# Rotary embedding on one core: the tables' loads moved to the GpSimd queue, and the fp32 head widened from two positions to four

## The chip, the core and the metric

The kernel runs on one core of one Trainium2 chip. The time is in device microseconds of one execution; the figure before is the median of three runs, 317.81 us (317.26 to 318.22). Engines are named as in the profile: DVE is VectorE, ACT is ScalarE, POOL is GpSimd, SP is SyncE. DMAs are issued by SP (queue q1, "hardware_dynamic", in the profile) and by POOL (queue q0, "software_dynamic"); both queues' packets run on the same 16 DMA engines.

## What is computed

An interleaved rotary embedding of x with 8 batches, 2048 positions, 16 heads and 64 elements per head, all float32 in HBM. The tables cos and sin have 2048 x 32 elements.

```python
x_pairs = x.reshape(batch, seq_len, num_heads, head_dim // 2, 2)
x1 = x_pairs[..., 0]
x2 = x_pairs[..., 1]
out1 = x1 * cos - x2 * sin
out2 = x1 * sin + x2 * cos
out = np.stack([out1, out2], axis=-1)
```

x is 67.1 MB and so is the output; each table is 0.26 MB.

## The kernel before

One batch is one tile of 128 partitions. Partition p holds 16 consecutive positions (K = 16) of 1024 elements each, so its row in HBM is 64 KB of float32. The tile `xt` in SBUF is bfloat16: the load (L56, `load`) and the store (L59, `store`) are DMAs issued by POOL which cast on the way, 64 KB of float32 on one side and 32 KB of bfloat16 on the other. There are five such tiles (NX = 5), for eight batches.

`rotate(b, k0, k1)` does the arithmetic on positions k0 to k1 of batch b with three DVE instructions: x times the sine table into the scratch tile `qt` (L74), x times the cosine table in place (L75), and the sum with the pairs of `qt` swapped (L80). The tables `s_tab` and `c_tab` are made once from `sin_sb` and `cos_sb` by three short DVE instructions (L93 to L95), the sine with the alternating sign.

The first positions of batch 0 go another way: SP loads them as float32 into the staging tile `head` (L84), and ACT casts them into the first tile (L91). HEAD is the number of these positions. Load 0 on POOL's queue brings the others. The last four positions of the last batch (TAIL = 4) go out in the same manner: ACT casts them to float32 (L118) and SP stores them (L119). `head`, `tail` and every `qt` share one buffer (tag "work").

The order is written out by hand. SP issues the head, then cos, then sin. POOL issues loads 0 to 4 without waiting. Then it goes batch by batch: store b waits for the rotation of batch b. After store 0, POOL runs a copy of one element (L106, `mark`) that reads the tile of load 4 and so waits for its landing; stores 1 and later are issued behind it. From batch 1 on, a load of batch b + 4 follows store b; it reuses the tile of batch b - 1 and waits on POOL until that batch's store has landed. So the issues run: loads 0 to 4, store 0, mark, store 1, load 5, store 2, load 6, store 3, load 7, stores 4 to 7. The last store leaves out the tail, and ACT's one-element copy (L117) holds the tail back until store 6 has landed.

In terms of rows: a transfer over 128 partitions puts eight rows on each of the 16 DMA engines. A row of a plain load is 64 KB on the HBM side, of load 0 it is 56 KB, of the head 8 KB, of a table 2 KB, of the tail 16 KB. Beside its 128 rows each transfer has 16 short completion packets, one for each engine: 16 transfers on POOL's queue give 16 x 144 = 2304 packets.

Of the kernel before, what the change touches and what calls it, by code (L numbers as in the profile page):

```python
# [2 lines left out]

# [4 lines left out]


@with_exitstack  # L10
def kernel(
    ctx: ExitStack,
    tc: tile.TileContext,
    x: bass.AP,
    cos: bass.AP,
    sin: bass.AP,
    out: bass.AP,
):
    nc = tc.nc
    fp32 = mybir.dt.float32  # L20
    bf16 = mybir.dt.bfloat16
    mult = mybir.AluOpType.mult
    add = mybir.AluOpType.add

    B, S, H, D = x.shape
    P = 128
    K = S // P
    KP = 16
    D2 = D // 2
    HD = H * D  # L30
    NX = 5
    HEAD = 2
    TAIL = 4


    x_t = x.rearrange("b (p k) h d -> b p k (h d)", p=P, k=K)
    out_t = out.rearrange("b (p k) h d -> b p k (h d)", p=P, k=K)
    cos_t = cos.rearrange("(p k) c -> p (k c)", p=P, k=K)
    sin_t = sin.rearrange("(p k) c -> p (k c)", p=P, k=K)

    consts = ctx.enter_context(tc.tile_pool(name="consts", bufs=1))
    xpool = ctx.enter_context(tc.tile_pool(name="xpool", bufs=NX))
    stage = ctx.enter_context(tc.tile_pool(name="stage", bufs=1))

    cos_sb = consts.tile([P, K * D2], fp32)
    sin_sb = consts.tile([P, K * D2], fp32)
    c_tab = consts.tile([P, K, D], bf16)
    s_tab = consts.tile([P, K, D], bf16)

    mark = consts.tile([1, 1], bf16)  # L50
    tiles = {}

    def load(b, k0=0):
        if b not in tiles:
            tiles[b] = xpool.tile([P, K, HD], bf16, name="xt")
        nc.gpsimd.dma_start(out=tiles[b][:, k0:], in_=x_t[b, :, k0:])  # L56

    def store(b, k1=K):
        nc.gpsimd.dma_start(out=out_t[b, :, :k1], in_=tiles[b][:, :k1])  # L59

    def rotate(b, k0, k1):
        nk = k1 - k0
        xp = tiles[b][:, k0:k1]
        qt = stage.tile([P, KP, HD], bf16, name="qt", tag="work")

        def rows(a):
            return a.rearrange("p k (h e) -> p k h e", h=H, e=D)

        def tab(a):
            return dataclasses.replace(  # L70
                a, offset=a.offset + k0 * D, ap=[a.ap[0], [D, nk], [0, H], [1, D]]
            )

        nc.vector.tensor_tensor(out=rows(qt[:, :nk]), in0=rows(xp), in1=tab(s_tab), op=mult)  # L74
        nc.vector.tensor_tensor(out=rows(xp), in0=rows(xp), in1=tab(c_tab), op=mult)  # L75
        q_swap = dataclasses.replace(
            qt, offset=qt.offset + 1, ap=[qt.ap[0], [2, nk * HD // 2], [-1, 2]]
        )
        x3 = xp.rearrange("p k (a j) -> p (k a) j", j=2)
        nc.vector.tensor_tensor(out=x3, in0=x3, in1=q_swap, op=add)  # L80

    with tc.manual_schedule():
        head = stage.tile([P, TAIL, HD], fp32, name="st", tag="work")
        nc.sync.dma_start(out=head[:, :HEAD], in_=x_t[0, :, :HEAD])  # L84
        nc.sync.dma_start(out=cos_sb, in_=cos_t)
        nc.sync.dma_start(out=sin_sb, in_=sin_t)
        load(0, HEAD)
        for b in range(1, NX):
            load(b)

        nc.scalar.copy(out=tiles[0][:, :HEAD], in_=head[:, :HEAD])  # L91
        s2 = s_tab.rearrange("p k (i j) -> p (k i) j", j=2)
        nc.vector.tensor_copy(out=s2[:, :, 0], in_=sin_sb)  # L93
        nc.vector.tensor_scalar_mul(s2[:, :, 1], sin_sb, -1.0)  # L94
        nc.vector.tensor_copy(  # L95
            out=c_tab.rearrange("p k (i j) -> p (k i) j", j=2),
            in_=cos_sb.to_broadcast([P, K * D2, 2]),
        )
        for b in range(B):
            if b == 0:  # L100
                rotate(b, 0, HEAD)
                rotate(b, HEAD, KP)
            else:
                rotate(b, 0, KP)
            if b == 1:
                nc.gpsimd.tensor_copy(out=mark, in_=tiles[NX - 1][:1, K - 1, :1])  # L106
            if b < B - 1:
                store(b)

            if b >= 1 and b - 1 + NX < B:  # L110
                load(b - 1 + NX)
        store(B - 1, K - TAIL)

        tail = stage.tile([P, TAIL, HD], fp32, name="st", tag="work")
        nc.scalar.copy(out=tiles[B - 2][:1, 0, :1], in_=tiles[B - 1][:1, K - 1, :1])  # L117
        nc.scalar.copy(out=tail, in_=tiles[B - 1][:, K - TAIL :])  # L118
        nc.sync.dma_start(out=out_t[B - 1, :, K - TAIL :], in_=tail)  # L119


# [1 line left out]
_INS = ['x', 'cos', 'sin']  # L123
_OUTS = [((8, 2048, 16, 64), 'float32')]


# [23 lines left out]
```

## Time and profile before

| | before |
|---|---|
| median of the runs | 317.81 us (317.26 to 318.22) |
| span of the profiled execution | 315.5 us |
| bytes read from and written to HBM | 67.63 MB and 67.11 MB, 427 GB/s over the span |
| DVE busy | 210.3 us, 67% of the span |
| ACT busy, POOL busy | 6.9 us, 11.7 us |
| head issued, landing after | 0.74 us, 4.7 us |
| cos issued, landing after | 1.16 us, 13.4 us |
| sin issued, landing after | 1.63 us, 31.7 us |
| load 0 issued, landing after | 1.24 us, 22.3 us |
| first DVE instruction | 33.38 us |
| store 0 issued | 61.93 us |
| L74, L75, L80 on a whole batch | 8.69 us each |
| tail issued, landing after | 299.08 us, 15.5 us |

The profiler records one execution. Times of issue are taken from its timeline; "landing" is the time from issue until the semaphore of the transfer shows it complete. In the view of the DMAs, a stretch of time can be given, and it then counts the packets that start there, with their bytes on the writing side and the time they take as a share of 16 engines over that stretch. A share can be over 100% where long packets start in a short stretch.

### The profile page before, as it was taken

The numbers are of one execution on the slowest core, as the hardware profiler recorded it, in microseconds if no ns is written. First come the engines' busy times: TensorE is split into PE (matmuls) and PEld (weight loads), VectorE is DVE, ScalarE is ACT, GpSimd is POOL, SyncE is SP. The second block draws the span as 40 slices with busy tenths as digits, with TensorE's granted clock in tenths as the row PEclk, the third lists the DMA queues.
The fourth block names the chain that finished last, engine by engine and source line by source line (L and its number), as shares of the span: only waits on it lengthen the run. The fifth ranks groups of instructions, "written<-read, shape, count | busy, mean of one in ns | idle before, by whom it ended". The sixth has DMA issues, their size and how long they took to land.

```text
span 315.5 us, 125 instructions
## 1 busy us (share of the span) xinstructions
DVE 210.3 (67%) x30; ACT 6.9 (2%) x4; POOL 11.7 (4%) x21
## 2 busy tenths in 40 slices
DVE  0000799999999999999999993899509994000000
ACT  4000000000000000000000000000000000000400
POOL 3000000000000301010000100000000000000000
DMA  9899999999999999999999999999999999999997
GB/s 279 184 261 206 199 220 245 199 199 253 212 199 266 399 449 482 399 332 245 220 399 399 399 199 199 399 532 266 199 241 490 399 399 490 440 399 399 432 432 332
DMA packets 2880, 101.71 MB, mean 322 GB/s; under 512 B 320, under 2 KB 320, under 8 KB 576
## 3 DMA queue, kind: packets, MB, share of 16 engines
q0 software_dynamic: 2304, 98.04, 97.1%
q1 hardware_dynamic: 576, 3.67, 3.0%
HBM read 67.63 MB, written 67.11 MB: 427 GB/s over the span
## 4 chain that ended last, share of the span: by engine, by line
another core or an unknown queue 91%; DMA 1%; ACTq 1%; ACT 1%; issue 0%
DMA st<-in_x_dram 1%; ACTq L145 1%; ACT xt L91 1%; ACT xt L117 0%; ACTq L117 0%
## 5 line engine op out<-in xcount | busy, mean ns | idle before, releaser
L74 DVE TENSOR_TENSOR qt<-xt,s_tab 128x16384 bf16<-128x16384 bf16 (+2 forms) x9 | 69.7, 7743 | 19.1 <-DMA xt<-in_x_dram 18.8
L75 DVE TENSOR_TENSOR xt<-xt,c_tab 128x16384 bf16<-128x16384 bf16 (+2 forms) x9 | 69.7, 7743 | 0.4
L80 DVE TENSOR_TENSOR xt<-xt,qt 128x16384 bf16<-128x16384 bf16 (+2 forms) x9 | 69.7, 7744 | 0.3
L93 DVE CAST s_tab<-sin_sb 128x512 bf16<-128x512 f32 x1 | 0.5, 453 | 33.4 <-DMA sin_sb<-in_sin_dram 33.4
L59 POOL DMA_DIRECT2D out_dram<-xt x8 | 4.3, 534 | 139.9 <-DVE xt L80 139.9
L56 POOL DMA_DIRECT2D xt<-in_x_dram x8 | 4.4, 560 | 72.8 <-DMA out_dram<-xt 72.0
L117 ACT COPY xt<-xt 1x1 bf16<-1x1 bf16 x1 | 0.2, 192 | 288.0 <-DMA out_dram<-xt 288.0
L106 POOL COPY mark<-xt 1x1 bf16<-1x1 bf16 x1 | 2.9, 2929 | 39.6 <-DMA xt<-in_x_dram 39.6
L118 ACT CAST st<-xt 128x4096 f32<-128x4096 bf16 x1 | 3.6, 3598 | 0.0
L91 ACT CAST xt<-st 128x2048 bf16<-128x2048 f32 x1 | 1.9, 1897 | 3.4 <-DMA st<-in_x_dram 3.4
L91 ACT ACT_TABLE_LOAD x1 | 1.3, 1283 | 0.7 <-PEq L134 0.7
L95 DVE CAST c_tab<-cos_sb 128x1024 bf16<-128x1024 f32 x1 | 0.7, 683 | 0.0
L94 DVE TENSOR_SCALAR s_tab<-sin_sb 128x512 bf16<-128x512 f32 x1 | 0.4, 444 | 0.0
L134 POOL MEMSET const-float32-0.0<- 128x1 f32 x1 | 0.1, 100 | 0.2 <-issue 0.2
L134 POOL MEMSET const-bfloat16-1.0<- 128x1 bf16 x1 | 0.1, 102 | 0.0
L134 POOL MEMSET const-float32-1.0<- 128x1 f32 x1 | 0.1, 100 | 0.0
L134 POOL MEMSET const-uint8-127<- 128x1 uint8 x1 | 0.1, 100 | 0.0
## 6 DMA issues: line engine op xcount, KB each, us to landing
xt<-in_x_dram POOLq DMA_DIRECT2D x7, 4096.0 KB, 57.6
out_dram<-xt POOLq DMA_DIRECT2D x1, 6144.0 KB, 47.8
xt<-in_x_dram POOLq DMA_DIRECT2D x1, 3584.0 KB, 22.3
out_dram<-st SPq DMA_DIRECT2D x1, 2048.0 KB, 15.5
st<-in_x_dram SPq DMA_DIRECT2D x1, 1024.0 KB, 4.7
cos_sb<-in_cos_dram SPq DMA_DIRECT2D x1, 256.0 KB, 13.4
sin_sb<-in_sin_dram SPq DMA_DIRECT2D x1, 256.0 KB, 31.7
out_dram<-xt POOLq DMA_DIRECT2D x7, 70.1
```

What stands on the lines that cost most here:

```text
L56: nc.gpsimd.dma_start(out=tiles[b][:, k0:], in_=x_t[b, :, k0:])
L59: nc.gpsimd.dma_start(out=out_t[b, :, :k1], in_=tiles[b][:, :k1])
L74: nc.vector.tensor_tensor(out=rows(qt[:, :nk]), in0=rows(xp), in1=tab(s_tab), op=mult)
L75: nc.vector.tensor_tensor(out=rows(xp), in0=rows(xp), in1=tab(c_tab), op=mult)
L80: nc.vector.tensor_tensor(out=x3, in0=x3, in1=q_swap, op=add)
L91: nc.scalar.copy(out=tiles[0][:, :HEAD], in_=head[:, :HEAD])
L93: nc.vector.tensor_copy(out=s2[:, :, 0], in_=sin_sb)
L94: nc.vector.tensor_scalar_mul(s2[:, :, 1], sin_sb, -1.0)
L95: nc.vector.tensor_copy(out=c_tab.rearrange("p k (i j) -> p (k i) j", j=2), in_=cos_sb.to_broadcast([P, K * D2, 2]),)
L106: nc.gpsimd.tensor_copy(out=mark, in_=tiles[NX - 1][:1, K - 1, :1])
L118: nc.scalar.copy(out=tail, in_=tiles[B - 1][:, K - TAIL :])
L145: with _tile.TileContext(nc) as tc:
```

## The change

Two things are changed. HEAD goes from 2 to 4, so that the head's rows are 16 KB and load 0's are 48 KB, ACT's cast covers four positions, and batch 0 is rotated as positions 0 to 4 and 4 to 16. And the loads of cos and sin are issued by POOL, after load 0 and ahead of loads 1 to 4, where before SP issued them behind the head. SP then issues the head alone until the tail at the end.

```diff
     HD = H * D
     NX = 5
-    HEAD = 2
+    HEAD = 4
     TAIL = 4
...
         head = stage.tile([P, TAIL, HD], fp32, name="st", tag="work")
         nc.sync.dma_start(out=head[:, :HEAD], in_=x_t[0, :, :HEAD])
-        nc.sync.dma_start(out=cos_sb, in_=cos_t)
-        nc.sync.dma_start(out=sin_sb, in_=sin_t)
         load(0, HEAD)
+        nc.gpsimd.dma_start(out=cos_sb, in_=cos_t)
+        nc.gpsimd.dma_start(out=sin_sb, in_=sin_t)
         for b in range(1, NX):
             load(b)
```

## The prediction

> **What bounds the kernel.** I first read the page's slices and queue totals. The DMA line shows the 16 engines full from the first slice to the last, and the two queues' shares add up to 97.1% + 3.0%. No compute engine comes near: DVE works 67% of the span and is done at about 263 us.
>
> ```profile
> DVE  0000799999999999999999993899509994000000
> DMA  9899999999999999999999999999999999999997
> q0 software_dynamic: 2304, 98.04, 97.1%
> q1 hardware_dynamic: 576, 3.67, 3.0%
> ```
>
> Next the waits, to see who is kept waiting by what, and then the timeline of POOL, which issues nearly every transfer.
>
> ```profile
> DVE s_tab L93 <- DMA sin_sb<-in_sin_dram: 33.4, 1, 33.4
> POOL mark L106 <- DMA xt<-in_x_dram: 39.6, 1, 39.6
> ...
> 61.93 0.54 POOL L59 DMA_DIRECT2D out_dram<-xt  x1 [57.89 <-DVE xt L80]
> 102.11 2.93 POOL L106 COPY mark<-xt 1x1 bf16<-1x1 bf16 x1 [39.64 <-DMA xt<-in_x_dram]
> 104.98 0.54 POOL L59 DMA_DIRECT2D out_dram<-xt  x1
> 121.68 0.53 POOL L56 DMA_DIRECT2D xt<-in_x_dram  x1 [16.17 <-DMA out_dram<-xt]
> ```
>
> The 33.4 us that DVE waits for sin look like the prize, but they are not on the path. Store 0 is issued at 61.93, behind loads 1 to 4 in q0's order. Load 4 lands at 102.1, and store 0, the only other work queued, lands at 121.68, that is 19.6 us later: the time one whole batch takes. So store 0 sat ready for 40 us, and DVE could be 40 us later, or any amount earlier, without moving it. From there on each batch costs the same: stores 4, 5 and 6 end a stretch from 237.26 to 295.28, 58.02 / 3 = 19.34 us each; loads 1 to 2 land 19.35 us apart (issues at 1.91 and 2.45, landing 41.1 and 59.9 later). The end is therefore the start of the stream plus the work of all packets in it. Only what happens before load 4 lands can change, and it moves the end one for one.
>
> **How an engine's time is spent at the start.** Asking the DMA view for short stretches gives packets by the time at which they start; share times stretch times 16 engines over packets is the length of one.
>
> ```profile
> q1 hardware_dynamic: 99, 0.81, 98.1%
> q1 hardware_dynamic: 35, 0.07, 87.2%
> q0 software_dynamic: 16, 0.46, 96.8%
> q1 hardware_dynamic: 16, 0.03, 4.4%
> q0 software_dynamic: 16, 0.52, 243.2%
> q1 hardware_dynamic: 26, 0.43, 99.3%
> q0 software_dynamic: 15, 0.49, 310.1%
> ```
>
> In order: 2.5 to 4.5 us, the head's 8 KB rows, 0.981 x 2 x 16 / 99 = 0.317 us each. 5.0 to 5.2, the tables' 2 KB rows back to back, 0.872 x 0.2 x 16 / 35 = 0.080 us (33 of the 35 are table rows, so 0.097 by count). 16.0 to 18.2, load 0 beside cos: each engine takes one 56 KB row (2.13 us) and one 2 KB row (0.097 us) in turn, 2.2 us a pair. 37 to 38, plain loads, 64 KB rows at 2.43 us. 311 to 312, the last store's 16 KB rows on the SP queue, 0.611 us. 98 to 99, the last packets of load 4, 3.3 us instead of 2.43: a single hitch of 0.9 us, whose cause no row shows. Every size runs close to one rate, 64 KB in 2.42 us.
>
> The turns explain sin's lateness: with load packets in q0, each 2 KB row on the SP queue waits out one large row. That is also why they cost little: an engine is never empty.
>
> **The change part by part**, per DMA engine, eight rows of every transfer each, from the first SP packet (about 2.0 us, mean over the engines) to the end of load 4.
>
> 1. Head of 4 positions. Removed: 8 rows of 8 KB, 8 x 0.317 = 2.54 us. Added: 8 rows of 16 KB at the tail's price, 8 x 0.611 = 4.89 us. Net +2.35. Low bound for 16 KB: the pace of 64 KB, 0.605; high bound, twice an 8 KB row, 0.634. So +2.30 to +2.53.
> 2. Load 0 shrinks from 56 to 48 KB rows: 8 x 8 KB, at the load pace exactly one 64 KB row, -2.42 us (bounds -2.41 from the spacing, -2.43 from the packet). With part 1: -0.07, bounds -0.13 to +0.12. The same bytes cross; only the queue differs.
> 3. The tables. Before, 16 rows per engine: some 5 in the gap between head and load 0 at 0.08 to 0.097, 11 in turn with load rows at about 0.09 (the pair of 2.2 us less the 2.11 that a 56 KB row takes at the load pace) or 0.06 (beside 64 KB rows: 2.47 less 2.41). Sum about 5 x 0.09 + 8 x 0.09 + 3 x 0.06 = 1.35 us. After, all 16 back to back in q0 between load 0 and load 1: 16 x 0.097 = 1.55. Bounds: 16 x 0.06 = 0.96 and, if the hardware queue's pace does not carry over, 16 x 0.12 = 1.92 (0.65 us from the last head row to the first load row for some 5.5 table rows). Net +0.2, bounds -0.4 to +0.6.
> 4. Two more transfers in q0, so two more ends of a transfer. At the ends of loads 1 to 3 none is seen: the 16 completion packets and the next load's 16 first rows start in the same stretch (42 to 43 us). The other end is the hitch of 0.9 us where load 4 meets store 0. I take 0.1 each, near the first row because these are loads followed by loads; bounds 0 and 1.8 for both.
> 5. POOL issues two more DMAs between load 0 and load 1, at 0.56 us each; loads 1 to 4 are issued 1.1 us later, the last at some 5.2 us instead of 4.04. Load 0 keeps the engines until about 21 us. Nothing; without that cover it would be 1.1 us. SP loses two issues (0.42 each), ahead of nothing. Should load 0's first packet, now at 5.35 on average, come 1.1 us later, the larger head alone fills the engines to 2.0 + 4.89 = 6.9.
> 6. ACT's copy of the head (L91) goes from 1.9 to 3.6 us, the time of the same size in L118; rotations of 4 and 12 positions replace 2 and 14, for the same total. The head now shares its engines with 48 KB rows from 5.35 on: about 5.3 of its 8 rows are done, the rest wait out one load row each, 2.7 x 2.4, so it lands near 12.5 us. Load 0 lands near 22, sin near 24, and DVE starts some 9 us earlier than 33.4. All of this lies under the queue of loads that ends at 102; cover gone, the ACT copy would cost 1.7 us.
>
> The queue's price deserves a rule that speaks against the change. The rows above show no gap at a load's end on q0. The Trainium skill, "DMA: Bandwidth & Descriptors", section "Anatomy of one DMA - SWDGE (gpsimd) path", gives each GpSimd DMA a fixed 2.0 us beside its bytes, mostly the receipt of the last write. If the tables paid it in a row with the loads, an estimate by that page is 4 us more for the two, near 322 us. The rows disagree: 19.35 us from load to load, the pace of the packets alone, leaves no room for such a cost between queued transfers.
>
> **Sum.** -0.07 + 0.2 + 0.2 = +0.3 us. The profiled span is 315.5 us, and the median of the runs is 317.81, 2.3 above it, the launch's share that the change doesn't touch. 317.81 + 0.3 = 318.1. From the bounds: -0.13 - 0.4 + 0 = -0.5, to 0.12 + 0.6 + 1.8 = +2.5.
>
> **Rivals.**
> - The tables drag (slower). Place: q0 between load 0 and load 1, 16 short rows with nothing on the SP queue to fill in, and two ends of transfers. For it: the hitch at 98 us and the dip to 22.1% share at 4.8 us where head gives way to cos; against it: clean ends at loads 1 to 3. It decides from the point where parts 3 and 4 exceed 1.0 us together; with 1.92 - 1.35 + 0.9 for one hitch, +1.5: 319.3 us.
> - The start gains (faster). Larger rows fill the early gap better, the tables run at 0.06, and the hitch at load 4 (0.9 us, shown once) doesn't return: -0.5 - 0.9 = -1.4, 316.4 us. Against it: the hitch lies where reads turn to writes, which the change leaves.
> - DVE's 9 us count (much faster). If the wait for sin were on the path, the time would fall toward 309 us. Against it: store 0 waits 40 us in the queue, and at 19.34 us a batch, 16 batches' worth of bytes take 309.4 us alone, before a start of 2.0, the 0.5 MB of tables, and 2.3 around the span.
> - It doesn't do what it says: the head is not sped up by being alone, since load 0's rows alternate with it. Likely, and the time is that of the forecast.
>
> **Numbers.** What a measurement here can tell from no change is about 0.3%, 0.95 us: 316.86 to 318.76. The forecast, including the last rival, 0.60; the tables drag 0.26; the start gains 0.11; DVE counts 0.03. The forecast's own range, with the runs' spread of half a us, is 317.2 to 318.9. For 8 in 10 I go from 316.7, inside the gain, to 319.5, past one hitch. Slower 0.27 (the drag and the forecast's upper edge), faster 0.14, same 0.59.
>
> **What would show it.** Sin landing near 24 us and the first DVE instruction with it, load 1 landing within 1 us of 43.0, load 4 within 1 us of 102.1, store 0 still landing 19.6 us after it: then the steps hold. A gap of more than 0.1 us per table row, or empty engines between load 0's last row and load 1's first, shows the drag. The prediction is wrong altogether if the pace of 19.34 us per batch changes, or if load 0 begins so late that the engines stand empty before it.

## The result

In the first comparison, 21 runs of each, the changed kernel took 317.31 us (317.12 to 317.51) and the kernel before 317.75 us (317.26 to 318.45): a ratio of 0.9983, 95% interval 0.9977 to 0.9989. That is inside the 0.3% called "no change" in the prediction and inside its range, but it is 0.44 us on the faster side, where the sum had +0.3 us. Five later comparisons on the same two kernels gave 0.9999, 1.0001, 1.0000, 0.9991 and 0.9991. The changed kernel stood between 317.29 and 317.43 us in all six; it is the kernel before that moved, from 317.31 to 317.75.

The profile after, first the page's slices and queue totals (digits are tenths of a slice; queues give packets, MB, share of 16 engines):

```profile
DVE  0009999999999999999879960799509994000000
DMA  7999999999999999999999999999999999999997
q0 software_dynamic: 2464, 98.04, 96.7%
q1 hardware_dynamic: 288, 4.19, 3.4%
```

The engines are as full as before, the shares add up to 100.1% again, and the span is 315.5 us, the same as that of the profile before. DVE starts a slice and more earlier and stands idle later instead. The waits (total, times, longest) and POOL's timeline say where:

```profile
POOL mark L106 <- DMA xt<-in_x_dram: 49.2, 1, 49.2
DVE qt L74 <- DMA xt<-in_x_dram: 28.5, 3, 12.6
DVE s_tab L93 <- DMA sin_sb<-in_sin_dram: 23.8, 1, 23.8
```

```profile
52.40 0.54 POOL L59 DMA_DIRECT2D out_dram<-xt  x1 [47.27 <-DVE xt L80]
...
102.18 2.06 POOL L106 COPY mark<-xt 1x1 bf16<-1x1 bf16 x1 [49.24 <-DMA xt<-in_x_dram]
104.18 0.54 POOL L59 DMA_DIRECT2D out_dram<-xt  x1
...
122.05 0.53 POOL L56 DMA_DIRECT2D xt<-in_x_dram  x1 [17.34 <-DMA out_dram<-xt]
```

In the kernel before, the line of the waits of L74 for loads was

```profile
DVE qt L74 <- DMA xt<-in_x_dram: 18.8, 2, 12.4
```

DVE's wait for sin shrank from 33.4 to 23.8 us, and its waits for loads grew from 18.8 to 28.5 us: the 9.6 us it gained at the start it gave back, to a tenth, further on. Store 0 is issued 9.5 us earlier and changes nothing, because load 4 lands at 102.18 (before: 102.11) and store 0 lands after it, at 122.05 (before: 121.68).

The issues of the first loads, with KB each and the time to landing:

```profile
xt<-in_x_dram POOLq DMA_DIRECT2D x1, 3072.0 KB, 21.2
st<-in_x_dram SPq DMA_DIRECT2D x1, 2048.0 KB, 14.5
...
cos_sb<-in_cos_dram POOLq DMA_DIRECT2D x1, 256.0 KB, 21.3
sin_sb<-in_sin_dram POOLq DMA_DIRECT2D x1, 256.0 KB, 21.4
```

Issued at 0.73, the head lands at 15.2 us, where before it landed at 5.4: alone on its queue, it waits for load 0's rows all the same. Cos and sin, issued by POOL at 1.90 and 2.44, land right behind load 0, at 23.2 and 23.8 us.

Short stretches of the DMA view, packets by their start: 3.5 to 5.1 us, 16.3 to 18.1 us and 21.9 to 22.9 us.

```profile
q1 hardware_dynamic: 45, 0.74, 110.8%
q0 software_dynamic: 16, 0.39, 101.6%
DMA packets 124, 0.40 MB, mean 397 GB/s; under 512 B 27, under 2 KB 27, under 8 KB 124
q0 software_dynamic: 124, 0.40, 99.7%
```

The head's 16 KB rows take 1.108 x 1.6 x 16 / 45 = 0.630 us, load 0's 48 KB rows 1.016 x 1.8 = 1.83 us. Between load 0 and load 1 come the tables: of 124 packets 27 are completions and 97 are table data, 0.40 MB, which makes 4 KB each. On POOL's queue two 2 KB rows are counted as one packet; that is why the queue has 2464 packets, 2304 + 2 x (64 + 16), and not 2 x 144 more. A packet takes 16 / 97 = 0.165 us with the completions in it, 0.082 us for 2 KB.

### The profile page after: what moved, and what is told of

Its sections match the earlier page's. It is cut to its first block, busy times and chain, and to the rows that moved or that the text cites. A ratio compares the mean times of both kernels' runs of the same rounds, so it can differ in the third digit from the quotient of the medians.

```text
span 315.5 us, 125 instructions
## 1 busy us (share of the span) xinstructions
DVE 210.4 (67%) x30; ACT 8.6 (3%) x4; POOL 11.9 (4%) x23
## 3 DMA queue, kind: packets, MB, share of 16 engines
q0 software_dynamic: 2464, 98.04, 96.7%
## 4 chain that ended last, share of the span: by engine, by line
another core or an unknown queue 88%; DMA 5%; ACT 1%; ACTq 1%; issue 0%
DMA st<-in_x_dram 5%; ACT xt L91 1%; ACTq L145 1%; ACT xt L117 0%; ACTq L117 0%
## 5 line engine op out<-in xcount | busy, mean ns | idle before, releaser
L74 DVE TENSOR_TENSOR qt<-xt,s_tab 128x16384 bf16<-128x16384 bf16 (+2 forms) x9 | 69.7, 7743 | 28.6 <-DMA xt<-in_x_dram 28.5
L93 DVE CAST s_tab<-sin_sb 128x512 bf16<-128x512 f32 x1 | 0.5, 455 | 23.8 <-DMA sin_sb<-in_sin_dram 23.8
L91 ACT CAST xt<-st 128x4096 bf16<-128x4096 f32 x1 | 3.6, 3604 | 13.3 <-DMA st<-in_x_dram 13.3
L106 POOL COPY mark<-xt 1x1 bf16<-1x1 bf16 x1 | 2.1, 2057 | 49.2 <-DMA xt<-in_x_dram 49.2
## 6 DMA issues: line engine op xcount, KB each, us to landing
st<-in_x_dram SPq DMA_DIRECT2D x1, 2048.0 KB, 14.5
```

## The experiments

**The parts, one at a time.** First the changed kernel and three neighbours on one chip, where the kernel before took 317.36 us (33 runs).

The first is the changed kernel itself (no edit).

> The changed kernel once more, beside the parts on the same chip. 317.3 us by every theory (21 runs gave 317.31, the kernel before 317.75).

Measured: 317.29 us, ratio 0.9999 (0.9990 to 1.0008). The first comparison's gain did not return.

```diff
 # against the changed kernel
-    HEAD = 4
+    HEAD = 2
```

> Head of 2 positions, tables on the GpSimd queue. Theory of the cover: the SP queue's work must last until the GpSimd queue's first packet starts (5.1 to 5.9 us in both profiles). Here the SP queue holds only the head, which ended at about 4.75 us, so the engines stand empty for about 0.6 us and the time is 317.9 us, over that of the changed kernel and about that of the kernel before or above it. Rival of the short rows: the 2 KB rows on the SP queue, in turn with load rows, are what cost time, so this kernel is as fast as the changed one, 317.3. Rival of the wide rows: only the 16 KB rows gain, so this kernel stays at 317.75.

Measured: 317.37 us, ratio 1.0001 (0.9992 to 1.0010). In its trace load 0's first rows start between 5.0 and 6.0 us and the head's last rows up to about 5.6, so there was no gap between the two. In a later trace of the same kernel (its second comparison, below) the head ends earlier, and load 0 starts earlier with it, between 4.6 and 5.5 us: POOL's first rows follow the head and keep no fixed time, so the theory of the cover fails.

```diff
 # against the kernel before
-    HEAD = 2
+    HEAD = 4
```

> Head of 4 positions, tables still on the SP queue. Cover: the SP queue holds work until about 8.4 us (2.0 + 8 x 0.611 + 16 x 0.097), so the time is that of the changed kernel, 317.3. Short rows: 317.75, as before. Wide rows: 317.3. Sin should land near 40 us, later than before, at no cost.

Measured: 317.14 us, ratio 0.9994 (0.9985 to 1.0003). Sin became available to DVE later still, as this line of its waits shows, and it cost nothing:

```profile
DVE s_tab L93 <- DMA sin_sb<-in_sin_dram: 53.0, 1, 53.0
```

Waiting 20 us longer for sin than the kernel before, it was no slower: this is the plainest proof that DVE's start is not on the path.

```diff
 # against the changed kernel
-    HEAD = 4
+    HEAD = 8
...
-        head = stage.tile([P, TAIL, HD], fp32, name="st", tag="work")
+        head = stage.tile([P, HEAD, HD], fp32, name="st", tag="work")
```

> Head of 8 positions (32 KB rows), tables on the GpSimd queue. Cover: nothing left to gain, 317.3. Wide rows: the gain goes on, with each doubling some 0.4 us, so 316.9. Short rows: 317.3.

Measured: 317.31 us, ratio 0.9999 (0.9990 to 1.0008). Wider rows than 16 KB bring nothing to the median.

**Doses.** If small parts can't be told apart, larger ones can. On a second chip (the kernel before 317.33 us, the changed one, the last of this group, 317.43):

```diff
 # against the changed kernel
-    HEAD = 4
+    HEAD = 0
...
-        head = stage.tile([P, TAIL, HD], fp32, name="st", tag="work")
-        nc.sync.dma_start(out=head[:, :HEAD], in_=x_t[0, :, :HEAD])
         load(0, HEAD)
...
-        nc.scalar.copy(out=tiles[0][:, :HEAD], in_=head[:, :HEAD])
...
-            if b == 0:
-                rotate(b, 0, HEAD)
-                rotate(b, HEAD, KP)
-            else:
-                rotate(b, 0, KP)
+            rotate(b, 0, KP)
```

> No head at all: batch 0 is loaded whole on the GpSimd queue, the tables behind it, SP loads nothing at the start. Theory that the GpSimd queue's first packet cannot start before about 5.1 us whatever SP does: the engines are empty until then, load 1's first packet starts at 5.2 + 8 x 2.42 + 1.2 = 25.8 us instead of 23.1, and the time is 2.7 us over the changed kernel, 320.0 us. Rival: the head on the SP queue is what holds the first load back; then it starts near 3.5 us and the time is 318.3 us.

Measured: 318.31 us (318.25 to 318.40), ratio 1.0032 (1.0019 to 1.0044): 0.9 us over the changed kernel. That is the rival's figure, though the rival put the start of load 0 near 3.5 us. The DMA view from 2.5 to 3.25 us of this kernel:

```profile
q0 software_dynamic: 16, 0.52, 428.6%
```

All 16 engines start load 0's first row there, between 2.6 and 3.1 us, at least 2.5 us earlier than in the kernel before, and these first rows take 4.286 x 0.75 = 3.2 us instead of 2.43. So POOL's queue can start by 2.6 us; with a head on the SP queue its first rows wait, which is read from the two traces side by side. In the prediction 5.35 us was taken for the time at which POOL's queue becomes ready; it is the time at which it gets its first turn.

```diff
 # against the changed kernel
         nc.gpsimd.dma_start(out=sin_sb, in_=sin_t)
+        for r in range(3):
+            nc.gpsimd.dma_start(out=spare[:, r], in_=sin_t)
```

> The changed kernel with sin loaded three times more into a spare tile, on the GpSimd queue right behind sin: 24 more rows of 2 KB per engine and three more ends of a transfer, in series with the loads. At the plain pace of bytes (0.075 us a row, which the changed kernel's trace suggests) +1.8 us, 319.1. As the prediction priced them (0.097 a row and 0.1 an end) +2.6, 319.9. By the rival of the dragging tables (0.12 a row and up to 0.9 an end) +2.9 to +5.6, 320.2 to 322.9.

Measured: 319.03 us, ratio 1.0054 (1.0040 to 1.0067): 1.60 us over the changed kernel, 0.067 us for 2 KB with the ends of three transfers included. These are medians of 5 and 11 runs that spread over 0.3 us. In the trace load 1's last completion packet starts at 44.7 us instead of 42.7, which makes 0.083 us a row. Its trace from 22.0 to 24.5 us:

```profile
DMA packets 316, 1.04 MB, mean 415 GB/s; under 512 B 63, under 2 KB 63, under 8 KB 316
q0 software_dynamic: 316, 1.04, 103.4%
```

253 packets of 4 KB in 2.5 us on 16 engines, 0.158 us each and 415 GB/s. Nothing drags: by either figure the short rows with the ends of their transfers cost at most a tenth more than their bytes (0.076 us for 2 KB at the pace of a 64 KB row), far from the 0.12 us of the rival.

```diff
 # against the kernel with HEAD = 4 and the tables on SP
         nc.sync.dma_start(out=sin_sb, in_=sin_t)
+        for r in range(3):
+            nc.sync.dma_start(out=spare[:, r], in_=sin_t)
```

> Head of 4, tables on the SP queue, and the same three more loads of sin behind them on the SP queue: 24 more rows of 2 KB per engine, each in turn with a load row. Beside 64 KB rows they cost 0.06 us each by the prediction: +1.4 us over the head-only kernel (317.1), 318.6. At the plain pace of bytes +1.8, 318.9. If rows in turn are hidden in gaps of the other queue: 317.1.

Measured: 319.04 us, ratio 1.0052 (1.0039 to 1.0065). Against the head-only kernel (317.14 to 317.22 in its three comparisons, all on other chips) that is 1.8 to 1.9 us, 0.076 to 0.079 us a row: the plain pace of bytes here too, with the rows in turn between load rows. The same five loads of tables take 319.03 us on POOL's queue and 319.04 on SP's, on one chip: between the two queues these runs show nothing to choose.

> The changed kernel once more. If the first comparison's 0.17% is the kernel's own, it returns: the kernel before at about 317.75 and this at 317.3. If it belongs to that session, the ratio is 1.000 as in the second one.

Measured: 317.43 us, ratio 1.0001 (0.9992 to 1.0010).

**A side question, the 3.3 us rows at 98 us.**

```diff
 # against the changed kernel
                 rotate(b, 0, HEAD)
+                nc.scalar.copy(out=early, in_=tiles[0][:, 0])
+                nc.sync.dma_start(out=out_t[0, :, 0], in_=early)
...
-                store(b)
+                store(b, K, 1 if b == 0 else 0)
```

(`store` got a first position, k0, and `early` is a float32 tile of one position.)

> In every trace so far the last load rows before store 0 take 3.3 us instead of 2.43, at the first change from reading x to writing the output and at no later one. Here one position of batch 0 is cast by ACT and stored from SP at about 33 us, amid the loads, and store 0 leaves it out; the bytes are the same. If the very first write to the output is what takes 0.9 us, the rows at 98 us return to 2.43 us, and the time is 316.4 us if other packets hide it, 317.3 if they wait for it. If the cause lies where the queue turns from loads to stores, the 3.3 us stay at 98 us, and the time is 317.3 us.

Measured: 317.24 us, ratio 0.9997 (0.9988 to 1.0005), 0.17 us under the changed kernel on the same chip (317.41, below). The last rows of load 4, 99 to 100 us:

```profile
q0 software_dynamic: 16, 0.52, 286.1%
```

2.86 us, half of the excess gone. Neither reading holds as stated, and the cause of this hitch stays open. But its length is not 3.3 us in every trace, as the expectation has it. The same 16 rows in five other traces, in this order: 98 to 99 us in the tables-only kernel's first (a run of 316.93 us, the shortest on record); then 97.8 to 98.8 us in two of the changed kernel (runs of 317.10 and 317.50 us), in the profile of the kernel before, and in its first copy below (a run of 317.55 us):

```profile
q0 software_dynamic: 16, 0.52, 265.2%
q0 software_dynamic: 16, 0.52, 317.7%
q0 software_dynamic: 16, 0.52, 360.2%
q0 software_dynamic: 16, 0.52, 331.2%
q0 software_dynamic: 16, 0.52, 362.8%
```

That is 2.65, 3.18, 3.60, 3.31 and 3.63 us a row. In the two traces of the changed kernel 0.42 us more in the hitch go with 0.40 us more in the time, and its other four traces lie between them, with 3.32 to 3.44 us and runs of 317.26 to 317.44. So the hitch appears to lie on the path. It is in the traces of both kernels, and no run shows that the change bears on it.

**The long runs of the kernel before.** The expectations call them a tail; this has nothing to do with the last four positions, which the code calls `tail`. Two further comparisons of the head-only and the changed kernel on a third chip, and one more of the changed kernel on a fourth:

> The head of 4 with the tables on the SP queue, again. If its 317.14 was its own, 0.2 us below the others, it returns; if all orders of the same bytes cost the same, 317.3 and a ratio of 1.000.

Measured: 317.22 us, ratio 0.9995 (0.9986 to 1.0004).

> The changed kernel in one more session. Same bytes, same time: the ratio is 1.000 and the kernel before is at 317.3. If the kernel before has a slower mode on some chips, as in the first comparison, it is at 317.7 and the ratio is 0.998.

Measured: 317.41 us, ratio 1.0000 (0.9991 to 1.0009); the kernel before 317.31.

> The changed kernel in a fifth comparison, counting the first. If the two kernels are equal, the ratio is 1.000 and the kernel before stands at 317.3; if the kernel before has a slower mode that comes with the session, it may stand at 317.7 and the ratio at 0.998.

Measured: 317.36 us (317.16 to 317.48), ratio 0.9991 (0.9982 to 0.9999); the kernel before 317.56 (317.21 to 318.32). This made the runs themselves worth sorting: the kernel before had single runs well above its lowest ones, the changed kernel had none. So the next four asked whose long runs these are and what removes them. The limit of 317.6 us was chosen with these runs in hand; no run of the changed kernel lay above 317.52. The second and the third are the head-only and the tables-only kernels from above; the fourth changes the order on SP:

```diff
 # against the kernel before
-        nc.sync.dma_start(out=head[:, :HEAD], in_=x_t[0, :, :HEAD])
         nc.sync.dma_start(out=cos_sb, in_=cos_t)
         nc.sync.dma_start(out=sin_sb, in_=sin_t)
+        nc.sync.dma_start(out=head[:, :HEAD], in_=x_t[0, :, :HEAD])
```

> The kernel before against itself. Over five comparisons 31 of its 113 runs lay above 317.6 us, and none of 66 of the changed kernel. If it has a tail of its own, some of these runs lie above 317.6 as well, and a profile that falls among them shows where the extra 0.3 to 1 us goes; the ratio is 1.000. If the tail belongs to the place in the order of measurement and not to the kernel, no run of this copy has it and the ratio is near 0.999.

Measured: 317.25 us (317.09 to 317.55), ratio 0.9997 (0.9989 to 1.0006). No long run in the copy here.

> Head of 4, tables on the SP queue. If the tail comes from the tables on the SP queue, runs above 317.6 appear here; if from the head of 2 with the tables behind it, none, 317.2.

Measured: 317.22 us (317.07 to 317.60), ratio 0.9996 (0.9988 to 1.0005).

> Head of 2, tables on the GpSimd queue. If the tail comes from the small head, runs above 317.6 appear here; if it needs both the small head and the tables behind it on the SP queue, none, 317.4.

Measured: 317.43 us (317.28 to 317.62), ratio 1.0001 (0.9992 to 1.0010).

> The kernel before with cos and sin issued on the SP queue ahead of the head of 2. The same three transfers, in another order: the 2 KB rows run alone at the start and the 8 KB rows meet the first load rows. If the tail needs 2 KB rows on the SP queue while load 0 begins, it is gone, 317.3; if any SP work of this size makes it, it stays.

Measured: 318.86 us, single runs from 317.34 to 319.93, ratio 1.0042 (1.0020 to 1.0064). The same bytes on the same queues, and the single runs spread over 2.6 us, where those of the kernel before spread over 1.4. The expectation rested on load 0 starting at 5.1 us, after the tables; in this trace it starts between 2.9 and 3.7 us, among the last table rows, with one engine at 4.2 to 4.3. From there on the trace (of a run of 318.65 us) is told by the spread of the engines. First the changed kernel's packets that start from 101.0 to 101.5 and from 101.5 to 102.0 us, where load 4 ends:

```profile
DMA packets 21, 0.66 MB, mean 1311 GB/s; under 512 B 11, under 2 KB 11, under 8 KB 11
DMA packets 11, 0.39 MB, mean 786 GB/s; under 512 B 5, under 2 KB 5, under 8 KB 5
```

Then the kernel with the tables first, from 101.0 to 101.5, 101.5 to 102.0 and 103.0 to 103.5 us (there is nothing from 102 to 103), and POOL's line when its load 4 has landed:

```profile
DMA packets 16, 0.52 MB, mean 1049 GB/s; under 512 B 8, under 2 KB 8, under 8 KB 8
DMA packets 14, 0.46 MB, mean 918 GB/s; under 512 B 7, under 2 KB 7, under 8 KB 7
DMA packets 2, 0.07 MB, mean 131 GB/s; under 512 B 1, under 2 KB 1, under 8 KB 1
```

```profile
103.50 3.44 POOL L106 COPY mark<-xt 1x1 bf16<-1x1 bf16 x1 [30.41 <-DMA xt<-in_x_dram]
```

Packets under 512 B are completions, one for each engine. In the changed kernel all 16 start within 0.7 us. With the tables first, 15 of them are out by 102.0 us as well, and the last comes alone, 1.9 us after the first. The laggard is 1.3 us behind at the end of load 1 already, and still at the end of load 3; the rows at 98 us add 0.5, and it is still 1.9 behind at the end of store 6, at 296.2. All engines have the same rows to move, so what one loses it never makes up, and the end waits for it: the last completion packets start between 313.7 and 314.4 us on 15 engines and at 315.6 on one, and in the changed kernel between 313.6 and 314.4 on all 16. So the laggard accounts for the 1.3 us between this run and the changed kernel's 317.31.

> The kernel before as a candidate once more, beside the changed one on the same chip. The first such copy had no run of 11 above 317.6 us while the reference runs had 7 of 30. If again none, the tail belongs to the reference's place in the measurement, and copy and changed kernel both stand at 317.3; if some, to the kernel, and the copy's median lies 0.1 to 0.4 us over the changed kernel's.

Measured: 317.57 us (317.34 to 317.92), ratio 1.0003 (0.9994 to 1.0012). The copy has the long runs, four of 11 above 317.6 us, and lies 0.27 us over the changed kernel beside it. (In the earlier session the reference had 6 of 30 above 317.6 us, not the 7 of the expectation.)

> The changed kernel beside the copy of the kernel before: 317.35 us, no run above 317.6, by both readings; what tells them apart is the copy.

Measured: 317.30 us (317.10 to 317.55), ratio 0.9991 (0.9982 to 1.0000).

All runs together, counted above 317.6 us:

| kernel | runs | median us | above 317.6 us | highest us |
|---|---|---|---|---|
| before, reference and copies | 186 | 317.42 | 50 | 318.45 |
| tables only | 22 | 317.42 | 1 | 317.62 |
| head only | 33 | 317.22 | 0 | 317.60 |
| head of 8, tables on POOL's queue | 11 | 317.31 | 1 | 317.67 |
| changed | 77 | 317.34 | 0 | 317.55 |

The long runs belong to the kernel before; how many of them show differs with the session, from a copy with 0 of 11 to a first comparison with 16 of 21. Which part of the change takes them away is not settled. The head-only kernel had 0 of 33 where the reference had 13 of 90 in the same three sessions, which chance alone would give about once in 75 times. The tables-only kernel had 1 of 22 against 10 of 63, which chance would give about once in six, and the head of 8 had 1 of 11 against 4 of 33. None of these three was run in a session in which long runs were frequent.

What makes the long runs of the kernel before is open, since no profile fell on one of them: those taken were of runs up to 317.55 us. Two candidates stand. One is a lagging engine, which is shown for the kernel with the tables first; but in the traces of the kernel before the engines are within about 0.5 us of each other from the end of load 1 on. The other is the hitch at 98 us, which was 3.31 us in the profile of the kernel before and 3.63 and 3.68 in its two copies (runs of 317.55 and 317.46 us).

The head-only kernel had the lowest median each time it ran, but its three intervals against the kernel before all hold 1, and whether it is really 0.1 us below the changed kernel is not settled by these runs.

## Why the prediction was right and where it failed

In short: the queues, the pace of the bytes and the wait that doesn't count were right. Two steps failed. The first is the base of the sum: it took 2.3 us for the launch's share where the runs show 1.8, and so held for fixed the 0.5 us that the kernel before's long runs spend inside the span. The second is the price of the tables, which gave the sum its sign. That the time still lay in the forecast's range is luck in part: the range was wide enough for an error that it did not have in mind.

**What bounds the kernel.** Right. 9.6 us of DVE's wait vanished without effect, a wait 20 us longer cost nothing, and each 2 KB row added at the start moved the end by 0.067 to 0.079 us per engine. The rival in which DVE's 9 us count is refuted by the head-only kernel.

**Parts 1 and 2, head and load 0.** Right within their bounds: 8 x 0.630 = 5.04 us for the head where 4.89 was taken, 1.83 us for a 48 KB row. Net about +0.1 instead of -0.07. Heads of 2, 4 and 8 positions take the same time.

**Parts 3 and 4, the tables.** Mis-sized, and with them the sign of the sum. Predicted: 1.55 us in series on POOL's queue, 0.2 for two ends, against 1.35 on the SP queue, +0.4 in all. Measured: 16 x 2 KB at 0.082 us, ends included, 1.3 us on POOL's queue (by the medians with the added tables, 1.1), and at 0.076 to 0.079 us about 1.2 to 1.3 on SP's. The difference is about zero, and in the profiles load 4 lands 0.07 us later than before. What failed here was to carry the hardware queue's packet of 2 KB over to the other queue, where the packets are 4 KB, and to charge anything for an end of a transfer; the hitch at 98 us, used as the high bound of such an end, is not at the end of these loads: the trace shows it in its old place, at 98 us. The rival of the dragging tables falls with it.

**The rule about a fixed cost.** The Trainium skill, "DMA: Bandwidth & Descriptors", section "Anatomy of one DMA - SWDGE (gpsimd) path", gives each GpSimd DMA some 2.0 us beside its bytes. Queued behind one another, these transfers don't show it: three more transfers on POOL's queue cost 1.60 us together by the medians and 2.0 by the trace, where their bytes alone make 1.8 (24 rows at 0.076 us) and three times 2.0 us would be 6 us more.

**Part 6, what lies under the loads.** Load 0 at 22.4 us (near 22 predicted), sin at 23.8 (near 24), DVE 9.5 us earlier (some 9). The head landed at 15.2 and not near 12.5 us: about three of its rows were left at 5.5 us, as taken, but each waited out a 48 KB row and then took 0.62 us itself, so the last of them ended near 13; and the completion packet behind it waited out one more 48 KB row, to 14.5 to 14.9 us on 15 of the engines. No price for it, as predicted.

**Part 5, the first load row.** The number was right and its meaning wrong: without a head POOL's queue starts at 2.6 us, and behind a head of two with no tables after it, in one trace, at 4.6 to 5.5 us, as the head ends. This did no harm to the sum, since the engines had SP's rows to move until then.

**The base of the sum.** This is the step that failed in the direction. The prediction added its +0.3 us to the median 317.81 and took the 2.3 us between that and the profiled span for "the launch's share that the change doesn't touch". In all runs whose span is on record, of either kernel and from 316.93 to 319.93 us, the time is 1.7 to 1.8 us above the span. So a span of 315.5 us belongs to a run of about 317.3: the profile was of a run like the shortest of the three (317.26), and the other 0.5 us of the 2.3 were not launch but the kernel before's own longer runs, spent inside the span. On that base the sum comes out: 315.5 + 1.8 + 0.1 with parts 1 to 4 corrected is 317.4 us, and the changed kernel stood at 317.29 to 317.43 in all six comparisons. The 0.44 us of the first comparison are the long runs, which the changed kernel doesn't have; in the three comparisons where the kernel before shows few of them the two medians lie within 0.1 us, in the other three the change takes off 0.2 to 0.4 us. Why the kernel before has them stays open, as said above.

The rival "the start gains" named larger rows, cheaper tables and the hitch. The gain is real in those sessions, but none of the three reasons is shown: a head of 8 brings nothing to the median, the tables cost the same on either queue, and the hitch is in the changed kernel's traces as in the others.

## What to carry to other kernels

When the DMA engines are full from end to end and one queue holds the work in order, an earlier start of a compute engine is worth nothing, and so is moving a small transfer from one queue to another: it costs its bytes either way. Before adding a change to a median, check that the profiled run is a run of that length: here time less span is 1.7 to 1.8 us in all runs, and a difference of 2.3 us was the sign that the profile showed a short run and the median a long one. Make such a sum per engine and ask which engine is last: in the kernel with the tables first, an engine that fell behind in the first microseconds stayed behind to the end. A difference of 0.1 to 0.2% needs several sessions and a look at the single runs: here the medians alone gave 0.17% once and nothing the next time, and only the count of long runs told the kernels apart.

## What the runs showed of the hardware that was not expected

- A queue's first turn depends on what another queue has begun: load 0's first row started at 2.6 to 3.1 us with nothing on the SP queue, at 2.9 to 3.7 us (one engine at 4.2 to 4.3) behind 2 KB rows, at 5.1 to 5.7 us behind the head of the kernel before, at 4.6 to 5.9 us behind the same head with no tables after it, at 5.3 to 6.2 behind 16 KB rows and at 6.0 to 6.4 behind 32 KB rows, although it was issued at 1.24 or 1.25 us each time. Once both queues run, they take turns row by row. What sets the first turn was not tried.
- The same table load is 128 packets of 2 KB on the SP queue and 64 of 4 KB on POOL's. The Trainium skill, "DMA: Bandwidth & Descriptors", section "SWDGE vs HWDGE vs iDMA", says that a packet on the GpSimd path is preferably up to 4096 B; the 4 KB agree with it, the 48 and 64 KB rows of the casting loads, which the profile counts as one packet each, do not.
- An order of three small transfers on one queue changed the spread of single runs from under 1.4 us (kernel before) to 2.6 us (tables first).
- The last rows of the last load before the first store take longer than the 2.43 us of the others, by an amount that differs from trace to trace: 2.65 us a row in the trace of the shortest run, 3.18 to 3.68 in the traces of the kernel before and of the changed one. The cause is open.
